# First transfers of a two-layer encoder kernel: order of the first loads, idle products and the list of places

## The chip, the cores and the metric

The kernel runs on one core of a Trainium2 chip. The metric is the device time of one execution in microseconds (us). Before the change the median of three runs is 606.17 us (606.11 to 606.56). The core has five engines with a queue of instructions each: TensorE (PE in the profile, with its weight loads as PEld), VectorE (DVE), ScalarE (ACT), GpSimd (POOL) and SyncE (SP). Each takes its own instructions strictly in the order in which the program was written, and engines wait for each other by semaphores. Transfers between HBM and SBUF are issued by SP and, for the first two of this kernel, by ACT.

## The reference

x is 256 rows of 1024 numbers in fp32. Two layers follow each other, each made of a mixer and a channel sublayer:

```python
def mixer_sublayer(x, n1, w_in_l, ...):
    h = rms_norm(x, n1)
    proj = h @ w_in_l                      # 1024 x 2560
    ...                                    # three attention groups on slices of proj
    return x + mix @ w_out_l
def channel_sublayer(x, n2, w_gu, cw, cb, w_dn):
    h = rms_norm(x, n2)
    g, u = jnp.split(h @ w_gu, 2, axis=-1) # 1024 x 5632
    g = depthwise_conv_centred(g, cw, cb)
    return x + (jax.nn.gelu(g, approximate=False) * u) @ w_dn
```

## The kernel before

Every large product is made from split operands: an fp32 matrix w is held as `hi` (rounded to the PE's fp32r type, by an ACT copy) and `lo` = w - hi (by DVE), and a product is three matmuls, hi by hi, hi by lo and lo by hi (`mm3`). The first products of the program are x (transposed, times the gain of the first norm) by the first slice of `w_in`, called dq: 8 blocks of 128 rows of the weights (k = 0 to 7), for both halves of 128 rows of x (t = 0, 1), three matmuls of 128x384 each: 48 matmuls.

Weights come in units. Unit 0 is blocks k = 0 to 3 of dq, four transfers of one block of 192 KiB each (w0 to w3 below). Unit 1 is blocks k = 4 to 7, in two transfers of 384 KiB (u1a, u1b). Unit 2 (u2) is the first half of the next slice, dk, 768 KiB in one transfer, unit 3 its second half. `load` issues the transfers of a unit, `split` makes its hi and lo. In the order listings below the buffers of the weights are named wp_raw (as loaded), wp_hi and wp_lo; the hi and lo of x transposed are act_hT.

Before the first product x must be turned: `split_T` transposes x on PE (a matmul against the identity `ident`, which is itself loaded), ACT multiplies by the gain and rounds (`hT` hi) and DVE makes the lo. The gain comes from `gl0`, 16x128, which is loaded, transposed on PE against `ident` and copied by DVE (`gains_T`). So the first product needs five things loaded: block 0 of x, `gl0`, `ident` and w0, the last through ACT's copy. x is loaded in blocks of 128 columns of all 256 rows: x0 and x1 alone (by ACT), then in pairs, called here x23, x45 and x67. The table `START` lists these first transfers in the order in which the program records them. While they are under way PE is given products of a constant with itself, whose result nobody reads (`warmed`): `WARM` of them recorded first and `WARM_MORE` wherever PE is free.

The program is not executed as recorded. A class `Plan` records every operation (its number i counts from 0), and `Plan.order` writes the instructions out: again and again it takes, of the operations whose inputs are made by then, the one with the smallest (time it could start, rank, i). The rank is i plus the shifts of the `later` blocks, plus the number that the table `PLACES` gives for i, where it has one. The table's numbers move single operations forward (negative) or back. The times are the planner's own estimates; for the first transfers they are the constants of `LANDS`, taken by the place in `START`.

A transfer gets one of eight semaphores in turn, so that the ninth and each later one is issued only when the transfer eight before it has landed. That wait stands on the issuing engine, and everything behind it in that engine's queue waits too.

Of the kernel before, what the change touches and what calls it, by code (L numbers as in the profile page):

```python
# [11 lines left out]
F32 = mybir.dt.float32  # L12
# [6 lines left out]
P = 128  # L19
# [28 lines left out]


START = [  # L50
    ("act", "x", (0, 1)), ("sync", "g", 0), ("act", "x", (1, 1)), ("sync", "ident", 0), ("sync", "w", 0),
    ("sync", "w", 1), ("sync", "x", (2, 2)), ("sync", "w", 2), ("sync", "w", 3), ("sync", "x", (4, 2)),
    ("sync", "x", (6, 2)), ("sync", "g", 1), ("sync", "g", 2),
]


LANDS = (4100, 3300, 5300, 3450, 5800, 6450, 7250, 8200, 8900, 9800, 10700, 10750, 10800)


WARM, WARM_MORE, WARM_W = 13, 15, 256  # L60

SUM_ACT, SCALE_ACT = ("dq", "dk", "cq"), ("dk",)

# [166 lines left out]
def handover(a, b):  # L230
# [1 line left out]


PLACES = {
# [25 lines left out]
}  # L260


class Plan:
# [83 lines left out]
    def order(self):  # L347
# [7 lines left out]
        free = dict.fromkeys(("ACT", "DVE", "POOL", "SP"), 550.0)  # L355
# [73 lines left out]
        while len(done) < len(ops):  # L429
            best = None  # L430
            for e, r in ready.items():
                for i in r:
                    o = ops[i]
                    if e in opened:
                        if o.burst != opened[e]:
                            continue
                        at = at_of(o)
                    elif o.burst is not None:
                        at = at_of_burst(o.burst) if i == self.bursts[o.burst][0] else None
                    else:  # L440
                        at = at_of(o)
                    if at is not None and (best is None or (at, o.rank, i) < best):
                        best = (at, o.rank, i)
            at, _, i = best
            o = ops[i]
            e = o.engine.name
            ready[e].remove(i)
            done.append(i)
            gone[i] = True
            if o.burst is not None:  # L450
                opened[e] = o.burst
                if i == self.bursts[o.burst][-1]:
                    del opened[e]
            for t in o.tiles:
                if t.slot is None:
                    s = t.pool
                    s.given += 1
                    place = min(s.free)
                    s.free.remove(place)
                    t.since, t.slot = taken_at(place[0], ""), place[1]  # L460
            if e == "PE":
                pe = run_on_pe(o, at)
                end = pe[0] + o.ns + {"turn": 218, "side": 379}.get(o.kind, 163)
            else:
                free[e], end = at + o.ns, at + o.lat
            if o.method == "dma_start":

                ring = e if i < self.first_loads else "SP"
                end = max(at + 1360, wires.get(ring, 0.0))
                shared = 0.0  # L470
                if i < self.first_loads:
                    shared = o.size if ring == "ACT" else min(o.size, 120 * max(0.0, wires.get("ACT", 0.0) - end))
                wires[ring] = end + shared / 120 + (o.size - shared) / (280 if i < self.first_loads else 335)
                end = wires[ring] + 1000
                if i < self.first_loads:
                    end = LANDS[sum(p.method == "dma_start" for p in ops[:i])]
            for t in o.tiles:
                t.left -= 1
                t.until = max(t.until, end)
                t.last[e] = end  # L480
                if not t.left:
                    t.pool.free.append((t.until, t.slot))
            for j in o.after:
                a = ops[j]
                f = a.engine.name
                if e != "PE" or f != "PE":
                    a.at = max(a.at, end + (100 if o.method == "dma_start" else handover(e, f)))
                a.left -= 1
                if not a.left:
                    ready[f].append(j)  # L490
# [55 lines left out]
def encoder_kernel(  # L546
# [27 lines left out]
    act = pool("act", 2)  # L574
    small = pool("small", 4)
    psa = pool("psa", 4, space=bass.MemoryType.PSUM)
    psw = pool("psw", 4, space=bass.MemoryType.PSUM)
# [8 lines left out]
    ident = const.tile([P, P], F32, tag="ident", name="ident")  # L586
# [17 lines left out]

    warm = const.tile([P, P], mybir.dt.bfloat16, tag="warm", name="warm")
    nc.gpsimd.memset(warm, 1.0)
    wps = psw.tile([P, WARM_W], F32, tag="w", name="wps")

    def warmed(n):
        for _ in range(n):  # L610
# [136 lines left out]
    def split_T(srcs, hi, lo, k0, g, name):  # L747


        n = g.shape[1]  # L750
        for b in range(0, n, 2):
            m = min(2, n - b)
            ps = psw.tile([P, 2, S], F32, tag="w", name=f"pt_{name}_{b}")
            for i in range(m):
                k = b + i
                for t in range(NT):
                    nc.tensor.transpose(
                        ps[:, i, t * P : (t + 1) * P], srcs[t][:, k * P : (k + 1) * P], ident
                    )
            for i in range(m):  # L760
                k = b + i
                h, o = hi[:, k0 + k], lo[:, k0 + k]
                nc.scalar.activation(h, ps[:, i], AF.Copy, scale=g[:, k : k + 1])
                nc.vector.scalar_tensor_tensor(
                    o, ps[:, i], g[:, k : k + 1], h.bitcast(F32), ALU.mult, ALU.subtract
                )
# [795 lines left out]
```

## Time and profile before

| | us |
|---|---|
| median of 3 runs | 606.17 |
| the profiled execution | 606.79 |
| its span, first to last instruction | 604.9 |
| PE busy in it | 597.9 |
| first of the 48 dq matmuls starts | 7.50 |
| last matmul of the program ends | 601.41 |

Times in the trace count from the start of the span. A row of the timeline has the start, the duration, the engine, the line (nearly all work has the line of the planner's writer), the operation and its tiles, the number of instructions merged, and in brackets how long the engine had been idle and what it waited for. Of two merged matmuls the second starts before the first one's modelled end, so that the distance of starts says more than the duration.

### The profile page before, as it was taken

What the parts mean: (1) busy time and instruction counts of PE and PEld (TensorE: products, weight loads), DVE (VectorE), ACT (ScalarE), POOL (GpSimd) and SP (SyncE); (2) the same over time, 40 slices, a digit from 0 to 9 for tenths busy, and PEclk for the clock granted to TensorE, in tenths of its full rate; (3) what the DMA queues carried; (4) which work ended last, traced back from release to release, by engine and by line L of the source; (5) the groups of instructions that cost most, each with busy time, mean ns of one, the idle gap of its engine ahead of it and who ended that gap; (6) DMA issues with size and microseconds to landing.
All of it is one profiled execution on the core that took longest, in us unless ns stands there. A gap on an engine that the chain in (4) does not pass through costs nothing.

```text
span 604.9 us, 9691 instructions
## 1 busy us (share of the span) xinstructions
PE 597.9 (99%) x3432; PEld 510.1 (84%) x3432; DVE 462.7 (76%) x951; ACT 426.8 (71%) x1065; POOL 82.5 (14%) x126
## 2 busy tenths in 40 slices
PE   8999999999999999999999999999999999999997
PEld 6998787788888888888899988778888888888886
DVE  4798866889888887878877886557868686777775
ACT  6789999685666676666786998786766556565661
POOL 0733130114300000000023214421000000000000
PEclk9999999999999999999999999999999999999999
DMA  8994123664669899989464817844447374664511
GB/s 269 299 277 168 54 86 109 210 208 141 201 216 306 289 328 319 324 296 310 157 189 137 277 58 256 291 167 138 140 140 254 112 262 139 209 208 161 189 70 70
DMA packets 85218, 121.44 MB, mean 201 GB/s; under 512 B 9881, under 2 KB 69881, under 8 KB 85169
## 3 DMA queue, kind: packets, MB, share of 16 engines
q1 hardware_dynamic: 82896, 112.17, 57.1%
q0 software_dynamic: 1728, 8.39, 4.0%
q8 instruction: 27, 0.44, 0.3%
q10 hardware_dynamic: 544, 0.26, 0.1%
q14 instruction: 23, 0.18, 0.1%
HBM read 110.93 MB, written 9.88 MB: 200 GB/s over the span
## 4 chain that ended last, share of the span: by engine, by line
PE 93%; DMA 2%; issue 1%; DVE 1%; ACT 1%; POOL 1%; SPq 0%; POOLq 0%; DVEq 0%
PE psw_w L498 49%; PE psa_a L498 44%; DMA wp_hi<-dram_khi 1%; DMA wp_raw<-in_w_in_dram 1%; DVE act_z L498 1%; ACT act_hT L498 0%; DVE wp_lo L498 0%; ACT act_s2k L498 0%; ACT wp_hi L498 0%; POOL act_qc L498 0%; POOL act_kc L498 0%; DVE act_sw L498 0%; SPq L498 0%; POOL small_rstd L498 0%; POOL wp_lo L498 0%
## 5 line engine op out<-in xcount | busy, mean ns | idle before, releaser
L498 DVE TENSOR_TENSOR wp_lo<-wp_raw,wp_hi 128x512 fp32r<-128x512 f32 (+2 forms) x332 | 234.9, 736 | 42.3 <-ACT wp_hi L498 21.8
L498 ACT CAST wp_hi<-wp_raw 128x512 fp32r<-128x512 f32 (+2 forms) x332 | 203.0, 666 | 15.7 <-PE psa_a L498 5.6
L498 PE MATMUL psw_w<-act_hT,wp_hi 128*128 128x512 f32 x704 | 181.4, 392 | 0.1
L498 PEld LDWEIGHTS psw_w<-act_hT,wp_hi 128*128 128x128 f32 x704 | 128.6, 188 | 25.1 <-DVE act_hT L498 0.4
L498 PE MATMUL psa_a<-wp_hi,act_hT 128*128 128x384 f32 (+2 forms) x448 | 112.5, 334 | 1.3 <-ACT act_hT L498 1.3
L498 PEld LDWEIGHTS psw_w<-act_hT,wp_lo 128*128 128x128 f32 x704 | 99.0, 190 | 7.7 <-DVE wp_lo L498 0.2
L498 PE MATMUL psw_w<-act_hT,wp_lo 128*128 128x256 f32 x704 | 104.2, 282 | 0.0
L498 PEld LDWEIGHTS psa_a<-wp_hi,act_hT 128*128 128x128 f32 x448 | 77.7, 189 | 4.4 <-ACT act_hT L498 1.6
L498 ACT COPY act_s2k<-psw_w 128x256 f32<-128x256 f32 x88 | 32.5, 373 | 65.6 <-PE psw_w L498 65.5
L498 PE MATMUL psa_a<-wp_lo,act_hT 128*128 128x384 f32 (+2 forms) x224 | 74.6, 336 | 1.1 <-DVE wp_lo L498 1.1
L498 DVE TENSOR_TENSOR act_s2k<-psw_w,act_s2k 128x256 f32<-128x256 f32 x88 | 36.8, 421 | 42.8 <-ACT act_s2k L498 42.1
L498 PE MATMUL psa_a<-wp_lo,act_ch 128*128 128x512 f32 (+1 forms) x176 | 68.7, 393 | 0.0
L498 PE MATMUL psa_a<-wp_hi,act_cl 128*128 128x512 f32 (+1 forms) x176 | 68.3, 392 | 0.0
L498 PE MATMUL psa_a<-wp_hi,act_ch 128*128 128x512 f32 (+1 forms) x176 | 65.7, 393 | 0.0
L498 PEld LDWEIGHTS psa_a<-wp_lo,act_hT 128*128 128x128 f32 x224 | 42.2, 189 | 4.3 <-DVE wp_lo L498 2.3
L498 DVE SCALAR_TENSOR_TENSOR act_s2k<-act_s2k,act_cw,act_s2k 128x255 f32<-128x255 f32 x88 | 38.7, 498 | 0.8 <-ACT act_s2k L498 0.7
L498 PEld LDWEIGHTS psa_a<-wp_lo,act_ch 128*128 128x128 f32 x176 | 33.0, 188 | 7.2 <-DVE wp_lo L498 0.6
L498 PEld LDWEIGHTS psa_a<-wp_hi,act_cl 128*128 128x128 f32 x176 | 33.0, 188 | 7.1
L498 PEld LDWEIGHTS psa_a<-wp_hi,act_ch 128*128 128x128 f32 x176 | 32.7, 188 | 6.4
L498 POOL TENSOR_TENSOR small_rstd<-small_ms,const_mh 128x6 f32<-128x6 f32 (+2 forms) x26 | 33.5, 1287 | 15.9 <-DVE small_ms L498 14.3
L498 ACT ACTIVATE act_s2k<-act_s2k,act_cw 128x256 f32<-128x256 f32 x44 | 24.1, 595 | 15.5 <-DVE act_s2k L498 15.5
L498 ACT ACTIVATE act_s2k<-act_s2k 128x512 f32<-128x512 f32 x22 | 13.9, 632 | 28.6 <-DVE act_s2k L498 28.4
(127 smaller groups left out, 715.6 us busy)
## 6 DMA issues: line engine op xcount, KB each, us to landing
wp_raw<-in_w_gate_up_dram SPq DMA_DIRECT2D x44, 1024.0 KB, 5.2
wp_raw<-in_w_down_dram SPq DMA_DIRECT2D x22, 1024.0 KB, 4.9
wp_raw<-in_w_in_dram SPq DMA_DIRECT2D x14, 768.0 KB, 4.6
wp_raw<-in_w_in_dram SPq DMA_DIRECT2D x8, 1024.0 KB, 6.5
wp_raw<-in_w_out_dram SPq DMA_DIRECT2D x8, 768.0 KB, 6.4
dram_khi<-act_mixT_hi SPq DMA_DIRECT2D x4, 768.0 KB, 6.1
dram_klo<-act_mixT_lo SPq DMA_DIRECT2D x4, 768.0 KB, 9.7
wp_lo<-dram_klo POOLq DMA_DIRECT2D x4, 768.0 KB, 6.0
```

What stands on the lines that cost most here:

```text
L498: getattr(o.engine.real, o.method)(*map(real, o.args), **{k: real(v) for k, v in o.kw.items()})
```

## The change

`START` has the first block of the weights, w0, as SP's first transfer, ahead of `gl0` and `ident`; `LANDS` gives new constants for the planner. `WARM` goes from 13 to 11 and `WARM_MORE` from 15 to 8. The idle products write a PSUM bank of the pool `psa` instead of `psw`. The first four blocks of x are transposed into a PSUM bank each, instead of two blocks to a bank. The planner counts DVE as taken while POOL runs a `tensor_copy`. The list `PLACES` is a new one; only the entries that bear on the opening are shown.

```diff
 START = [
-    ("act", "x", (0, 1)), ("sync", "g", 0), ("act", "x", (1, 1)), ("sync", "ident", 0), ("sync", "w", 0),
+    ("act", "x", (0, 1)), ("sync", "w", 0), ("act", "x", (1, 1)), ("sync", "g", 0), ("sync", "ident", 0),
     ("sync", "w", 1), ("sync", "x", (2, 2)), ("sync", "w", 2), ("sync", "w", 3), ("sync", "x", (4, 2)),
...
-LANDS = (4100, 3300, 5300, 3450, 5800, 6450, 7250, 8200, 8900, 9800, 10700, 10750, 10800)
+LANDS = (3600, 3600, 4500, 3750, 3900, 5200, 5900, 6500, 7000, 7900, 8800, 8850, 8900)
...
-WARM, WARM_MORE, WARM_W = 13, 15, 256
+WARM, WARM_MORE, WARM_W = 11, 8, 256
...
 PLACES = {
-    47: 18, 57: -84, 81: -133, 85: -19, 89: -85, 93: 16, 145: 11, 157: -3, 158: -286, 159: -286, 160: -6, 164: 14,
...
+    76: -251, 77: -166, 78: -166, 80: -153, 82: -153, 120: 6, 137: 110, 159: -236, 160: -236, 161: -236, 189: -272,
...
             else:
                 free[e], end = at + o.ns, at + o.lat
+                if e == "POOL" and o.method == "tensor_copy":
+                    free["DVE"] = max(free["DVE"], at + o.ns)
...
-    wps = psw.tile([P, WARM_W], F32, tag="w", name="wps")
+    wps = psa.tile([P, WARM_W], F32, tag="a", name="wps")
...
         n = g.shape[1]
-        for b in range(0, n, 2):
-            m = min(2, n - b)
+        step = 1 if name == "n100" else 2
+        for b in range(0, n, step):
+            m = min(step, n - b)
```

With nine idle products fewer, operations 76, 77 and 78 of the changed program are the two transfers of unit 1 and the one of unit 2; 80 and 82 are the ACT copies of the first two blocks of unit 1. What the planner makes of it on SP, the first transfers, before (wp_raw_93 is unit 0, wp_raw_130 unit 1, wp_raw_145 unit 2, act_s2k the gains, and a row with x2 stands for two instructions):

```order
L498 DMA act_s2k_81<-in_norm_g_dram 16x128
L498 DMA const_ident_89<-in_c_ident_dram 128x128
L498 DMA wp_raw_93<-in_w_in_dram 128x384 x2
L498 DMA const_x_79<-in_x_dram 128x2x256
L498 DMA wp_raw_93<-in_w_in_dram 128x384 x2
L498 DMA const_x_79<-in_x_dram 128x2x256 x2
L498 DMA act_s2k_122<-in_out_norm_g_dram 16x128
L498 DMA act_s2k_122<-in_norm_g_dram 16x128
L498 DMA wp_raw_130<-in_w_in_dram 128x2x384 x2
L498 DMA wp_raw_145<-in_w_in_dram 128x4x384
```

And on SP in the changed program, from its first transfer (wp_raw_81 is unit 0, wp_raw_88 unit 1, wp_raw_97 unit 2):

```order
L501 DMA wp_raw_81<-in_w_in_dram 128x384
L501 DMA wp_raw_88<-in_w_in_dram 128x2x384 x2
L501 DMA wp_raw_97<-in_w_in_dram 128x4x384
L501 DMA act_s2k_101<-in_norm_g_dram 16x128
L501 DMA const_ident_105<-in_c_ident_dram 128x128
L501 DMA wp_raw_81<-in_w_in_dram 128x384
L501 DMA const_x_79<-in_x_dram 128x2x256
L501 DMA wp_raw_81<-in_w_in_dram 128x384 x2
L501 DMA const_x_79<-in_x_dram 128x2x256 x2
```

Besides w0, all of units 1 and 2 moved ahead of the gains, of `ident`, of w1 to w3 and of x23 to x67.

On ACT, the first work behind its two transfers and the load of its table, before (wp_hi_133 is unit 0, wp_hi_225 unit 1; CAST is the copy to hi, the ACTIVATE on const_x a sum of squares for the norm):

```order
L498 CAST wp_hi_133<-wp_raw_93 128x384
L498 ACTIVATE act_hT_138<-psw_w_116,const_gains_114 128x256 x2
L498 CAST wp_hi_133<-wp_raw_93 128x384
L498 ACTIVATE act_s2k_158,small_ssx_157<-const_x_79 128x512
L498 ACTIVATE act_s2k_169,small_ssx_157<-const_x_79 128x512
L498 CAST wp_hi_133<-wp_raw_93 128x384 x2
L498 ACTIVATE act_hT_138<-psw_w_155,const_gains_114 128x256 x2
L498 ACTIVATE act_hT_138<-psw_w_109,const_gains_114 128x256 x2
L498 ACTIVATE act_s2k_213,small_ssx_157<-const_x_79 128x512
```

And in the changed program at the same place (wp_hi_112 is unit 0, wp_hi_141 unit 1):

```order
L501 CAST wp_hi_112<-wp_raw_81 128x384
L501 ACTIVATE act_hT_131<-psw_w_120,const_gains_127 128x256
L501 ACTIVATE act_hT_131<-psw_w_125,const_gains_127 128x256
L501 CAST wp_hi_141<-wp_raw_88 128x384 x2
L501 CAST wp_hi_112<-wp_raw_81 128x384 x3
L501 ACTIVATE act_hT_131<-psw_w_149,const_gains_127 128x256
L501 ACTIVATE act_hT_131<-psw_w_116,const_gains_127 128x256
L501 ACTIVATE act_s2k_185,small_ssx_184<-const_x_79 128x512
L501 ACTIVATE act_hT_131<-psw_w_120,const_gains_127 128x256 x2
```

Two copies of unit 1 now stand ahead of those of w1 to w3, and the sums of squares behind them.

On PE the changed program has 16 idle products first, then the transposes of the gains, of x0 and, behind one idle product, of x1, two more idle products, and the first four real ones (k = 0, both halves of x); the transposes of x23 follow. Before, 14 idle products stood ahead of the transpose of the gains, 13 more between there and the first real product, and one later.

49 rows, old and new, of the table PLACES are left out of this document.

## The prediction

> **What bounds the kernel.** I read the page's busy times first, then what PE waited for, then the timeline of the opening.
>
> ```profile
> span 604.9 us, 9691 instructions
> PE 597.9 (99%) x3432; PEld 510.1 (84%) x3432; DVE 462.7 (76%) x951; ACT 426.8 (71%) x1065; POOL 82.5 (14%) x126
> PE psa_a L498 <- ACT act_hT L498: 1.3, 1, 1.3
> PE psa_a L498 <- DVE wp_lo L498: 1.1, 2, 0.9
> PE psw_w L498 <- POOL const_mh L498: 1.0, 1, 1.0
> ```
>
> PE is busy 597.9 of 604.9 us, and its waits (total us, times, longest) come to 3.4 us: 1.0 before the first idle product, 1.3 before the first real one, 1.1 in two waits on DVE. What PE does behind its first real product is fixed work, so the end moves with two things: when real products begin and how fast PE then runs. Nothing behind can repay more than 1.1 us and some tenths.
>
> ```profile
> 6.56 0.51 ACT L498 CAST wp_hi<-wp_raw 128x384 fp32r<-128x384 f32 x1 [3.56 <-DMA wp_raw<-in_w_in_dram]
> 6.98 0.84 ACT L498 ACTIVATE act_hT<-psw_w,const_gains 128x256 fp32r<-128x256 f32 x2
> 7.50 0.44 PE L498 MATMUL psa_a<-wp_hi,act_hT 128*128 128x384 f32 x1 [1.29 <-ACT act_hT L498]
> 18.17 0.23 ACT L498 ACTIVATE act_s2k<-psa_a 128x64 f32<-128x64 f32 x1 [0.53 <-PE psa_a L498]
> ```
>
> The first real product starts at 7.50, held by ACT, which was held by w0 until 6.56. ACT waits for the first finished half of dq until 18.17: 10.67 us from the first product to there.
>
> **The order of the transfers** is the term that decides. SP's issues, and for single transfers the time from issue to landing (last number, KB each):
>
> ```profile
> 0.73 0.40 SPq L498 DMA_DIRECT2D act_s2k<-in_norm_g_dram  x1
> 1.18 0.41 SPq L498 DMA_DIRECT2D const_ident<-in_c_ident_dram  x1
> 1.64 0.91 SPq L498 DMA_DIRECT2D wp_raw<-in_w_in_dram  x2
> wp_raw<-in_w_in_dram SPq DMA_DIRECT2D x1, 192.0 KB, 4.9
> 6.56 0.33 SPq L498 DMA_DIRECT2D act_s2k<-in_norm_g_dram  x1
> act_s2k<-in_norm_g_dram SPq DMA_DIRECT2D x1, 8.0 KB, 4.1
> 7.07 2.17 SPq L498 DMA_DIRECT2D wp_raw<-in_w_in_dram  x4
> wp_raw<-in_w_in_dram SPq DMA_DIRECT2D x1, 384.0 KB, 4.3
> ```
>
> So w0 lands at 1.64 + 4.9 = 6.54, the last gains (8 KB, issued 6.56) at 10.66, u1a (issued 7.07) at 11.37. Eight kilobytes need 4.1 us because all that SP issued before goes first. The change puts 192 + 768 + 768 KB (w0, units 1 and 2) ahead of `gl0` and `ident`, so `ident` waits for them. What is moved, in GB/s (the last number, 1000 KB per us):
>
> ```profile
> 1.00:2.00 1.00, 1.00 (x5) 0.70 (x6) 0.00 (x0) 0.28 (x1) 0.00 (x0) 1.00 0.11 32
> 2.00:4.00 2.00, 2.00 (x11) 1.18 (x8) 0.00 (x0) 1.00 (x1) 0.00 (x0) 1.00 0.95 222
> 4.00:6.00 2.00, 2.00 (x19) 1.76 (x18) 0.17 (x1) 0.00 (x0) 0.00 (x0) 1.00 0.83 230
> 6.00:8.00 2.00, 0.71 (x4) 0.46 (x3) 0.71 (x2) 1.44 (x4) 0.00 (x0) 1.00 1.01 340
> 8.00:10.00 2.00, 2.00 (x14) 1.93 (x13) 1.31 (x4) 2.00 (x7) 0.00 (x0) 1.00 0.99 327
> 10.00:12.00 2.00, 2.00 (x17) 1.80 (x16) 1.87 (x5) 1.99 (x6) 0.00 (x0) 1.00 0.96 328
> ```
>
> Up to `ident`, with x0 and x1 (2 x 128 KB on ACT's queue), gains 8 and `ident` 64, that is 2056 KB, or 2105 thousand bytes. By these rows 32 + 444 + 460 + 680 = 1616 are moved by 8.0, and 2105 at 9.5. Landing lags: w0 closes 532 thousand bytes, moved by 4.3 and landed at 6.54 (2.2 later); the last gains close 1925, moved by 8.95, landed 1.7 later; u1a closes 2318, moved by 10.15, landed 1.2 later. So `ident` lands at 9.5 + 1.2 to 1.7, **about 10.8**. From below: if the transfers ran from 2.0 on at the later 330, 2.0 + 2073/330 + 1.2 = 9.5. From above, with w0's lag: 11.7. Before, PE used `ident` at 4.02 (row below).
>
> Behind it come w1 (197 thousand bytes), x23 (262), w2, w3 (197 each), x45 and x67 (262 each): at 330 they land at about 11.4, 12.2, 12.8, 13.4, 14.2 and 15.0. The wait of each for the transfer eight before it (x67 for u2) ends ahead of these times.
>
> **From `ident` to the first product.** PE's clock matters here.
>
> ```profile
> 0.98 3.11 PE L498 MATMUL psw_w<-const_warm 128*128 128x256 bf16 x14 [0.98 <-POOL const_mh L498]
> 4.02 0.23 PE L498 MATMUL psw_w<-const_ident,act_s2k 16*128 16x16 f32 x1
> 4.63 0.71 PE L498 MATMUL psw_w<-const_warm 128*128 128x256 bf16 x5
> 5.18 0.38 PE L498 MATMUL psw_w<-const_ident,const_x 128*128 128x128 f32 x2
> 601.13 0.28 PE L498 MATMUL psw_w<-wp_hi,act_cl 128*128 128x256 f32 x1
> 603.40:604.40 1.00, 0.00 (x0) 0.00 (x0) 0.00 (x0) 0.00 (x0) 0.00 (x0) 1.00 0.00 0
> 604.60:604.90 0.30, 0.00 (x0) 0.00 (x0) 0.00 (x0) 0.00 (x0) 0.00 (x0) 0.58 0.00 0
> ```
>
> The first 14 idle products take (4.02 - 0.98)/14 = 0.217 us each, later ones (5.18 - 4.63)/5 = 0.11: PE runs at half speed for its first 3.1 us. At the end the granted clock (third number from the right) is 1.00 until 604.4 and partly low from 604.6, 3.0 to 3.5 us after the last product's end at 601.41. In the changed kernel the 16 idle products end near 0.98 + 14 x 0.217 + 2 x 0.11 = 4.2, and nothing can follow until 10.8: 6.6 us without work. So PE is slow again. The transpose of the gains (0.23), four of x (two in 0.38 above, which is 0.11 from start to start; 2 x 0.11 each when slow) and three idle products (0.217 each) take 0.23 + 0.88 + 0.65 = 1.8 us, and the first product starts at about **12.6**, 5.1 later. (ACT's hT of x0 is ready before, at 10.8 + 0.7 + 0.45.) From 10.8 another 3.1 us are slow, until 13.9; the 1.3 us of products in it do half their work: **+0.65**.
>
> On what the clock costs there is a page that differs in size. The Trainium skill, TensorE: Matmul & The Clock Gate, Part 1, gives a free-running window of 3.4 us: a whole busy window raises the clock, so the wait for it can be 3.4 to 6.8 us as the phase falls. By it this term would be 0.8 to 2.4 us and the sum 611.2 to 612.8, by the row 611.0; this trace has one such rise, after 3.1 us, and cannot show the spread.
>
> **Is anything later still?** ACT from its first hT on:
>
> ```profile
> L498 ACT CAST wp_hi<-wp_raw 128x384 fp32r<-128x384 f32 x12 | 5.6, 514 | 4.0 <-DMA wp_raw<-in_w_in_dram 4.0
> L498 ACT ACTIVATE act_hT<-psw_w,const_gains 128x256 fp32r<-128x256 f32 x8 | 3.5, 473 | 0.0
> L498 ACT ACTIVATE act_s2k<-const_x 128x512 f32<-128x512 f32 x4 | 2.5, 635 | 0.0
> 15.88 1.76 ACT L498 CAST wp_hi<-wp_raw 128x384 fp32r<-128x384 f32 x4 [0.44 <-DMA wp_raw<-in_w_in_dram]
> 16.06 0.51 PE L498 MATMUL psa_a<-wp_hi,act_hT 128*128 128x384 f32 x2
> 16.41 0.33 PE L498 MATMUL psa_a<-wp_lo,act_hT 128*128 128x384 f32 x1
> ```
>
> The same 24 instructions stand there, one CAST of them ahead (w0's, early now): 5.6 x 11/12 + 3.5 + 2.5 = 11.1 us, from 11.5 to 22.6, where before the last CAST of unit 2 ended at 17.64: 5.0 later. In ACT's queue the CASTs of w1 to w3 hold the hT of x23 until about 14.5, w3 having landed at 13.4. PE, from 12.6, needs 0.65 + 10.67 us to the end of the first half of dq: 23.9, so PE's sum and ACT's agree to within a microsecond, and PE's is the later. The early landing of units 1 and 2 gains nothing: they were not waited for long (0.44 above).
>
> **Other parts.** Nine idle products fewer cost nothing: all but one stood in a wait, and the wait is longer now. Separate banks for x0 to x3 and `psa` for the idle products cost nothing on PE: no instruction is added, and the banks are free until the first product. The new list moves work all along. What it can gain is the wait behind POOL's copy:
>
> ```profile
> 21.38 1.84 POOL L498 COPY act_nab<-act_few 28x1984 f32<-28x1984 f32 x1
> 21.93 3.38 DVE L498 TENSOR_TENSOR wp_lo<-wp_raw,wp_hi 128x384 fp32r<-128x384 f32 x4
> 23.69 0.45 PE L498 MATMUL psa_a<-wp_lo,act_hT 128*128 128x384 f32 x1 [0.88 <-DVE wp_lo L498]
> ```
>
> Four of DVE's lo take 3.38 us beside the copy, and PE waits 0.88. In the changed program the copy stands seven POOL instructions later, and the planner keeps DVE's work off it. Bounds: 0.9 gained (the wait is gone), 0.9 lost (a second such wait, as the opening's real times aren't those planned for). I take **-0.9**, as the list was made with that rule.
>
> **Sum.** Against the profiled execution's 606.79 (span 604.9 and 1.9 around it): 5.1 + 0.65 - 0.9 = +4.85, 611.6. The median of the runs is 0.6 below the profiled one, so the forecast is 606.17 + 4.85 = **611.0**.
>
> **Rivals.** (1) *Transfers under way share the engines*, so a small one overtakes. `ident`, SP's sixth issue at 0.73 + 5 x 0.45 = 3.0, would land as x0 did, 2.5 us after its issue:
>
> ```profile
> const_x<-in_x_dram ACTq DMA_DIRECT2D x2, 128.0 KB, 2.5
> ```
>
> That is 5.5; the first product would start near 6.6, 0.9 earlier, PE's clock would hold, and with -0.9 the time is 604.4. It decides below about 7.5 for the first product. Against it: the 8 KB that took 4.1. The Trainium skill, DMA: Bandwidth & Descriptors, Queues, rings and completion order, has each engine take descriptors in ring order, though a later one may finish its write first. 7%. (2) *The delay is repaid* to within 0.2%: `ident` would have to land by about 7.3, between the two cases, or PE save 3.6 us more where it waits 1.1. 3%, 606.5. (3) *The clock stays low* in the opening, because PE now waits between products for ACT: some 20 more of the 48 products at twice their 0.175 us ((16.41 - 16.06)/2, above) add 3.5, giving 614.5. 8%. (4) *The clock holds* through the gap: the first product at 11.9 (ACT's hT), no slow products: 4.4 - 0.9, 609.7. 12%. The forecast has 70%.
>
> **Range and chances.** Lower end: `ident` at 9.5 instead of 10.8 and the clock partly kept: 611.0 - 1.3 - 1.3 = 608.4. Upper: `ident` at 11.7 and no gain at POOL's copy, 611.0 + 0.9 + 0.9 = 612.8, and part of rival 3, 613.4. Outside are rivals 1 and 2 and most of 3, some 18%. A measurement can tell 0.2%, 1.2 us, from no change; faster 0.07, same 0.03, slower 0.90.
>
> **What would show it.** The gains and `ident` landing near 10.8 and the transpose of the gains right behind; an idle stretch of PE of over 6 us from about 4.2; a granted clock below 1.00 in 8 to 13; the first real product near 12.6; ACT's first sums of dq near 23.5; no PE wait of 0.9 on DVE beside POOL's copy. A first product before 7.5 would make the prediction wrong from its root.

## The result and the profile after

Timed side by side on one chip, the changed kernel takes 611.21 us (median of four, 611.08 to 611.87) and the one before 606.14 (605.53 to 606.56): a ratio of 1.0087, 95% interval 1.0069 to 1.0104, that is 4.2 to 6.3 us slower. The forecast was 611.0.

The page of the changed kernel, its span and the busy times:

```profile
span 609.3 us, 9680 instructions
PE 598.8 (98%) x3423; PEld 512.1 (84%) x3423; DVE 461.3 (76%) x951; ACT 424.4 (70%) x1065; POOL 80.4 (13%) x126
```

The span is 4.4 us longer, and PE is busy only 0.9 us longer although it has nine matmuls fewer. So PE waits more. All its waits (total us, times, longest):

```profile
PE psw_w L501 <- DMA const_ident<-in_c_ident_dram: 4.8, 1, 4.8
PE psa_a L501 <- POOL const_mh L501: 1.0, 1, 1.0
PE psa_a L501 <- DVE wp_lo L501: 0.7, 1, 0.7
PE psw_w L501 <- DVE act_z L501: 0.2, 1, 0.2
```

The 1.3 us for ACT's hT are gone, and 4.8 for `ident` stand in their place. The opening in the timeline (start, duration, engine, line, operation, tiles, count, idle time before):

```profile
0.73 1.89 SPq L501 DMA_DIRECT2D wp_raw<-in_w_in_dram  x4
2.66 0.50 SPq L501 DMA_DIRECT2D act_s2k<-in_norm_g_dram  x1
3.20 0.42 SPq L501 DMA_DIRECT2D const_ident<-in_c_ident_dram  x1
...
0.98 3.60 PE L501 MATMUL psa_a<-const_warm 128*128 128x256 bf16 x16 [0.98 <-POOL const_mh L501]
9.39 0.26 PE L501 MATMUL psw_w<-const_ident,act_s2k 16*128 16x16 f32 x1 [4.81 <-DMA const_ident<-in_c_ident_dram]
...
10.98 0.67 PE L501 MATMUL psa_a<-wp_hi,act_hT 128*128 128x384 f32 x1
11.45 0.52 PE L501 MATMUL psa_a<-wp_lo,act_hT 128*128 128x384 f32 x1
11.77 0.52 PE L501 MATMUL psa_a<-wp_hi,act_hT 128*128 128x384 f32 x1
...
13.03 0.95 PE L501 MATMUL psa_a<-wp_hi,act_hT 128*128 128x384 f32 x4
13.82 0.34 PE L501 MATMUL psa_a<-wp_lo,act_hT 128*128 128x384 f32 x1
...
22.47 0.22 ACT L501 ACTIVATE act_s2k<-psa_a 128x64 f32<-128x64 f32 x1 [1.80 <-PE psa_a L501]
...
605.48 0.28 PE L501 MATMUL psw_w<-wp_hi,act_cl 128*128 128x256 f32 x1
```

Against the rows of before: the first real product starts at 10.98 instead of 7.50 (+3.48), the first half of dq ends at 22.47 instead of 18.17 (+4.30), and the last matmul starts at 605.48 instead of 601.13 (+4.35). The whole loss is there after 22 us; behind, next to nothing is lost or repaid on balance. (The end of the first half of dq is read from ACT's first sum over it, `act_s2k<-psa_a`, as in the prediction.) The products from 11.45 on start 0.32 us apart, those from 13.03 on (13.82 - 13.03)/4 = 0.20: PE's clock was low until about 12.9. `ident` in the chain that ended last (start, duration):

```profile
3.20 6.05 DMA const_ident<-in_c_ident_dram
```

64 KB, issued at 3.20, landed at 9.25.

### The profile page after: what moved, and what is told of

It reads as the page before. It is cut to its first block, busy times and chain, and to the rows that moved or that the text cites. A ratio compares the mean times of both kernels' runs of the same rounds, so it can differ in the third digit from the quotient of the medians.

```text
span 609.3 us, 9680 instructions
## 1 busy us (share of the span) xinstructions
PE 598.8 (98%) x3423; PEld 512.1 (84%) x3423; DVE 461.3 (76%) x951; ACT 424.4 (70%) x1065; POOL 80.4 (13%) x126
## 4 chain that ended last, share of the span: by engine, by line
PE 92%; DMA 2%; DVE 2%; POOL 1%; issue 1%; ACT 1%; SPq 0%; POOLq 0%; ACTq 0%
PE psw_w L501 50%; PE psa_a L501 42%; DMA wp_lo<-dram_klo 1%; DMA const_ident<-in_c_ident_dram 1%; POOL small_rstd L501 1%; DVE wp_lo L501 1%; SPq L501 0%; DVE act_z L501 0%; DVE const_x L501 0%; ACT act_s2k L501 0%; ACT act_z L501 0%; POOL small_ms L501 0%; ACT wp_hi L501 0%; DVE act_sw L501 0%; POOL act_cdq L501 0%
## 5 line engine op out<-in xcount | busy, mean ns | idle before, releaser
L501 PE MATMUL psa_a<-wp_hi,act_ch 128*128 128x512 f32 (+1 forms) x176 | 68.3, 392 | 0.0
L501 DVE SCALAR_TENSOR_TENSOR act_s2k<-act_s2k,act_cw,act_s2k 128x255 f32<-128x255 f32 x88 | 37.2, 479 | 2.1 <-ACT act_s2k L501 2.0
L501 POOL TENSOR_TENSOR small_rstd<-small_ms,const_mh 128x6 f32<-128x6 f32 (+2 forms) x26 | 32.2, 1238 | 15.6 <-DVE small_ms L501 14.0
```

What stands on the lines that cost most here:

```text
L501: getattr(o.engine.real, o.method)(*map(real, o.args), **{k: real(v) for k, v in o.kw.items()})
```

## The experiments

Those that move transfers without a new plan do it where the instructions are written out; `made` is that order, and the operations named by number are moved ahead of another. For each the ratio to the kernel before is given; the kernel before had a median of 607.03 beside the first four, 606.33 beside the two with the undone opening's hole filled and with nine idle products fewer, and 606.2 beside the others.

**The kernel before, with only units 1 and 2 (and w0) ahead of the gains and `ident` on SP** (34 is w0, 85 to 87 the transfers of units 1 and 2):

```diff
-            for i in self.order():
+            made = [i for i in self.order() if i not in [34, 85, 86, 87]]
+            at = made.index(31)
+            made[at:at] = [34, 85, 86, 87]
+            for i in made:
```

> The kernel before with one thing moved: on SP w0 and units 1 and 2 are issued first, everything else in its old order, with its old list and 28 idle products. Theory A: ident lands near 9.3, the first real product starts near 11, the clock is low at first, and the time is 610.2 us (609.3 to 611.3), most of the change's loss. Rivals B and C: without fewer idle products and without the new list no loss, 606.1 (605.5 to 606.8).

1.0102 [1.0086, 1.0118]. From its timeline and its windows (window, its length, busy time of the engines, granted clock third from the right, DMA share, GB/s):

```profile
9.90 0.26 PE L501 MATMUL psw_w<-const_ident,act_s2k 16*128 16x16 f32 x1 [5.75 <-DMA const_ident<-in_c_ident_dram]
13.55 0.67 PE L501 MATMUL psa_a<-wp_hi,act_hT 128*128 128x384 f32 x1
```

```profile
7.50:10.80 3.30, 0.90 (x5) 0.83 (x6) 0.61 (x2) 0.00 (x0) 0.00 (x0) 0.50 1.08 379
10.90:14.20 3.30, 3.30 (x17) 2.66 (x15) 0.67 (x2) 1.55 (x4) 0.00 (x0) 0.50 0.89 285
```

The order of the transfers alone makes the whole loss and more (1.0102 where 610.2 us, some 1.007, were expected): the same wait for `ident`, and behind it the 13 idle products of before, now at half speed (clock 0.50), hold the first product until 13.55. From the use of `ident` to the first product it takes 3.65 us here and 1.59 in the changed kernel, which has three idle products there; ten idle products more at about 0.21 us account for the difference. By this estimate the fewer idle products spare the changed kernel some 2 us.

**The changed kernel without the three entries that move units 1 and 2 forward**, planned again:

```diff
-    76: -251, 77: -166, 78: -166, 80: -153, 82: -153, 120: 6, ...
+    80: -153, 82: -153, 120: 6, ...
```

> The changed kernel without the three entries of the list that move units 1 and 2 ahead. Theory A (the place of units 1 and 2 ahead of ident is the whole cost): ident lands near 3.9 instead of 9.25, the first real product starts at 5.0 to 5.6 (before 7.50, changed 10.98), PE's clock is full there, and the time is about 603.9 us (602.8 to 605.2), faster than both. Rival B (nine idle products fewer, so a cold PE, is the cost): the clock comes late here too and the time stays above 608. Rival C (the rest of the new list costs): 606.5 to 609.

1.0010 [0.9997, 1.0023]. The loss is gone. The gain that was expected is not there, though the opening is early. Its timeline:

```profile
6.36 0.44 PE L501 MATMUL psa_a<-wp_hi,act_hT 128*128 128x384 f32 x1
18.70 0.23 ACT L501 ACTIVATE act_s2k<-psa_a 128x64 f32<-128x64 f32 x1 [2.08 <-PE psa_a L501]
```

The first product is 1.14 us earlier than in the kernel before, the end of the first half 0.53 later: PE has waits in between (0.7 for ACT's hi, 0.4 for x) and work that the list places ahead.

**The changed kernel with the gains and `ident` right behind w0, units 1 and 2 behind these**, but still ahead of w1 to w3 and x23 to x67:

```diff
+            made = [i for i in self.order() if i not in [24, 25]]
+            at = made.index(76)
+            made[at:at] = [24, 25]
```

> The changed kernel with only the gains and ident (72 KB) issued right behind w0, units 1 and 2 still ahead of w1 to w3 and the rest of x. Theory A with the whole order as cause: the first real product starts near 5.3, but after four of them PE waits for x23, which lands at about 10.3 as in the changed kernel, so that only 1.2 to 2.2 us come back: 609.5 us (608.8 to 610.2). If ident alone is the cost, nearly all comes back: 606.5 to 607.3.

1.0083 [1.0065, 1.0102]: nothing gained, where 1.2 to 2.2 us were expected. In its timeline the wait has moved:

```profile
6.11 0.44 PE L504 MATMUL psa_a<-wp_hi,act_hT 128*128 128x384 f32 x1
...
11.51 1.12 PE L504 MATMUL psw_w<-const_ident,const_x 128*128 128x128 f32 x4 [4.43 <-DMA const_x<-in_x_dram]
```

Four products at 6.11, then 4.43 us for x23, which stands behind the same 1536 KB. In that wait the clock fell (0.50 from 10.8 to 14.2), so that the products behind it are slow as well, and the first half of dq ends at 22.58. So `ident` is only the first of the things that are late; what costs is that the two units go ahead of *anything* the first products need.

**The kernel before with the new `START` and `LANDS` only**, its old list kept and planned with them:

```diff
-    ("act", "x", (0, 1)), ("sync", "g", 0), ("act", "x", (1, 1)), ("sync", "ident", 0), ("sync", "w", 0),
+    ("act", "x", (0, 1)), ("sync", "w", 0), ("act", "x", (1, 1)), ("sync", "g", 0), ("sync", "ident", 0),
```

> The kernel before with the new START and LANDS alone, its own list, 28 idle products, old banks. Theory A: w0 as SP's first transfer is good in itself; first real product at 5.2 to 6.0, time 604.3 us (603.4 to 605.3). If w0 ahead of ident is itself what hurts, ident lands over a microsecond later and the time is 606 or more.

1.0052 [1.0035, 1.0069], expected faster: missed. The opening is early (first half of dq at 17.32, 0.85 before the old one), the last matmul at 604.70, 3.57 later. Of PE's waits that are new against the kernel before these are the longest:

```profile
PE psw_w L498 <- ACT act_s2k L498: 0.9, 2, 0.5
PE psa_a L498 <- DMA wp_hi<-dram_khi: 0.6, 1, 0.6
PE psa_a L498 <- ACT wp_hi L498: 0.6, 1, 0.6
PE psw_w L498 <- DMA const_x<-in_x_dram: 0.5, 1, 0.5
```

They are spread over the first 400 us. The list of numbers was made for the old times of the planner; with others it puts work in other places all along. The next run, which leaves the order as planned before, bears out that this costs more here than w0 first does. So a new plan can't tell what a new opening is worth.

**The kernel before with only w0 at the head of SP's queue**, written out otherwise as it was:

```diff
+            made = self.order()
+            for what, ahead_of in [([34], 31)]:
+                made = [i for i in made if i not in what]
+                at = made.index(ahead_of)
+                made[at:at] = what
...
```

> The kernel before as written out, with only w0 moved to the head of SP's transfers; nothing is planned anew. If the opening's gain is real and the loss of the replanned run (START alone) came from its list no longer fitting: first real product near 6.4, first half of dq done at 17.0 to 17.5 (before 18.17), ratio 0.998 to 0.999. If w0 first is no gain: first half of dq at 18.2 and ratio 1.000; if it hurts by itself, ratio over 1.002 and 610 us as in the replanned run.

1.0015 [1.0003, 1.0028]. In the profiled execution PE is early for a long time (first product at 6.71, first half of dq at 17.48, 0.69 early), and then:

```profile
395.39 0.30 PEld L506 LDWEIGHTS psa_a<-wp_hi,act_mixT_hi 128*128 128x128 f32 x2 [1.34 <-DMA wp_hi<-dram_khi]
```

The weight load waits 1.34 for a block of weights that POOL reloads. In the kernel before it stood at the same place, at nearly the same time, with a shorter wait:

```profile
395.45 0.30 PEld L498 LDWEIGHTS psa_a<-wp_hi,act_mixT_hi 128*128 128x128 f32 x2 [0.58 <-DMA wp_hi<-dram_khi]
```

The reload in the chain that ended last (start, duration), before, in this run, and in the run with nine idle products fewer (below):

```profile
389.10 6.30 DMA wp_hi<-dram_khi
388.28 7.07 DMA wp_hi<-dram_khi
390.22 7.07 DMA wp_hi<-dram_khi
```

POOL issued it 0.82 earlier, and it took 0.77 longer, so that it landed no sooner; the last matmul starts at 601.00, 0.13 early. In that profile the early start is used up there. The longer transfer is no consequence of being early: it takes 7.07 us also where PE comes late. Why is open. By the ratio the kernel is 0.9 us slower than the one before (medians 607.69 and 606.20), which the trace doesn't explain: its eleven executions fall into two groups, five from 606.05 to 606.57, the profiled one among them, and six from 607.69 to 608.72, and no trace was taken of the second. It stays open.

**The changed kernel with the opening undone in the written order**: units 1 and 2 behind the first loads again, ACT's and DVE's work on u1a behind that on w1 to w3, nothing planned anew.

```diff
+            made = self.order()
+            for what, ahead_of in [([80, 81, 82, 83], 129), ([76, 77, 78], 79)]:
+                made = [i for i in made if i not in what]
+                at = made.index(ahead_of)
+                made[at:at] = what
...
```

> The changed kernel as written out, with only this moved: on SP units 1 and 2 stand behind the other first transfers again (the order of START), and ACT's and DVE's first two pieces of unit 1 behind w1 to w3 and x23 to x67. All other instructions keep the changed kernel's order, so that the list's effect on the rest stays. Theory A (the whole loss is the place of units 1 and 2): first real product at 5.8 to 6.5, first half of dq done near 17 instead of 22.5, ratio to before 0.997 to 0.999. Rival C (the new list loses elsewhere, as the replanned run of the changed list might say): ratio 1.000 to 1.004 with the opening as early.

1.0028 [1.0017, 1.0039]; last matmul at 602.79, 2.69 earlier than in the changed kernel. Some 3 us (2.7 by the profile, 0.0059 or 3.6 us by the ratios) come back with nothing but these seven operations moved. More was expected by theory A: the first product comes at 7.27 and the first half of dq ends at 20.15, not near 17. What remains shows in its timeline:

```profile
0.99 3.60 PE L509 MATMUL psa_a<-const_warm 128*128 128x256 bf16 x16 [0.99 <-POOL const_mh L509]
5.68 0.25 PE L509 MATMUL psw_w<-const_ident,act_s2k 16*128 16x16 f32 x1 [1.10 <-DMA const_ident<-in_c_ident_dram]
...
7.74 0.52 PE L509 MATMUL psa_a<-wp_lo,act_hT 128*128 128x384 f32 x1
8.06 0.52 PE L509 MATMUL psa_a<-wp_hi,act_hT 128*128 128x384 f32 x1
```

PE has a hole of 1.10 us, and its products are 0.32 apart behind it.

**The same with that hole filled**: the sixteenth idle product six times.

```diff
-                getattr(o.engine.real, o.method)(...)
+                idle += o.method == "matmul" and o.args[1].dtype == mybir.dt.bfloat16
+                for _ in range(6 if idle == 16 and o.method == "matmul" and ... else 1):
+                    getattr(o.engine.real, o.method)(...)
```

> The opening of the change undone as in the run that undid it (units 1 and 2 and ACT's two pieces behind again; that left 1.0028 [1.0017, 1.0039]), and now the sixteenth idle product of the list 6 times, 5 more of about 0.22 us, so that PE bridges the 1.1 us for which it waited for ident there. Theory (what was left of the loss is the clock, which came full only at 9.83): full clock by 4 to 5 us, first product of weights at 7.0 to 7.5, end of the first half of dq 18.9 to 19.4 where it was 20.15, last matmul 601.5 to 602.1 where it was 602.79; ratio 1.0005 to 1.0020. Rival (the rest of the loss is the new list, made for other starts): clock early too, but the last matmul within 0.3 of 602.79 and ratio 1.0025 to 1.0035.

1.0016 [1.0007, 1.0025]. Its timeline:

```profile
0.98 3.83 PE L512 MATMUL psa_a<-const_warm 128*128 128x256 bf16 x21 [0.98 <-POOL const_mh L512]
...
6.21 0.44 PE L512 MATMUL psa_a<-wp_hi,act_hT 128*128 128x384 f32 x1
6.49 0.34 PE L512 MATMUL psa_a<-wp_lo,act_hT 128*128 128x384 f32 x1
6.67 0.35 PE L512 MATMUL psa_a<-wp_hi,act_hT 128*128 128x384 f32 x1
...
19.59 0.23 ACT L512 ACTIVATE act_s2k<-psa_a 128x64 f32<-128x64 f32 x1 [2.09 <-PE psa_a L512]
```

The clock is high for the first products (0.18 apart), and the first one comes 1.06 us earlier than without the filling; of that only 0.56 arrive at 19.59 and 0.58 at the last matmul (602.21). But this pair doesn't show that the filling did it. PE uses `ident` at 5.08 here and at 5.68 there, though SP issues it at 1.63 in both; that is 0.60 of the 1.06. And the clock rose here before the two programs differ: the starts of the idle products are 0.21 apart up to 3.73 and 0.11 from 3.89 on, while the added ones begin behind 4.0; without the filling all sixteen were slow (3.60/16 = 0.225), and the rise came at 9.83. The intervals of the two ratios overlap. PE, early now, waits for x:

```profile
PE psw_w L512 <- DMA const_x<-in_x_dram: 1.2, 1, 1.2
```

The ratio is the theory's, the last matmul lies between theory and rival, and neither is shown. About 1.1 us against the kernel before stay, and all of it is lost by 19.59 (18.17 before): the new order asks for x sooner than it lands and waits 0.4 for ACT's hi. How much of it is the list's and how much the other parts of the change (the order of `START`, the banks), no run separates.

**The changed kernel with its own hole filled**: the sixteenth idle product 49 times, so that PE works up to `ident`.

```diff
+                for _ in range(49 if idle == 16 and o.method == "matmul" and ... else 1):
```

> The changed kernel with the 16th idle product of PE issued 49 times instead of once, so that PE stays busy until ident is there (48 more at 0.11 to 0.21 us, to 9.4 to 11). Theory: about 1 us of the loss is PE's low clock behind the gap; with it full from ident on, the first half of dq is done 0.5 to 1.5 us earlier than 22.47 and the ratio to before falls from 1.0087 to 1.006 to 1.008. If the clock costs nothing there, because ACT's 10 us of work set the pace, the ratio stays at 1.0087 and dq at 22.3 to 22.5.

1.0066 [1.0052, 1.0079]; first product at 10.60, those behind it 0.17 apart, and:

```profile
21.68 0.23 ACT L504 ACTIVATE act_s2k<-psa_a 128x64 f32<-128x64 f32 x1 [1.61 <-PE psa_a L504]
```

That is 0.79 us earlier than in the changed kernel, 0.62 at the last matmul (604.86). So the low clock is 0.6 to 0.8 us of the 4.35 in the profiles; the intervals of the two ratios overlap. Here too the clock rose before the programs differ (at 3.8), but that alone would not have kept it: with units 1 and 2 first in the kernel before it rose at 4.0 and fell again in the wait for `ident`.

**The kernel before with nine idle products fewer** (one of those ahead of `ident`, eight of those behind):

```diff
+            idle = [i for i in made if self.ops[i].method == "matmul" and ...]
+            gone = set(idle[13:14] + idle[18:26])
+            for i in [i for i in made if i not in gone]:
...
```

> The kernel before with nothing changed but nine idle products fewer: one of the fourteen ahead of ident and eight of those between x's transposes and the first products. Theory (the shorter run of idle products is no part of the 5 us so long as the clock still comes full before the first products, and the first product waits for hT and w0's parts and not for PE): first product 7.2 to 7.5 where it was 7.50, full clock by 3.9 to 7.3, last matmul within 0.5 of 601.13; ratio 0.999 to 1.001. Rival (the clock goes down in the gap that they leave, or comes up a period of 3.4 us later): products 0.32 apart until 7.3 or longer, last matmul 0.5 to 1.3 later, ratio 1.001 to 1.002.

1.0004 [0.9995, 1.0013]: no difference in the medians. But the profiled execution is the slowest of its eleven (608.50, the others 605.46 to 607.39), and its windows say why in part:

```profile
3.80:7.20 3.40, 1.50 (x12) 1.00 (x11) 0.64 (x2) 1.01 (x3) 0.00 (x0) 1.00 0.88 277
...
7.30:10.60 3.30, 3.30 (x12) 3.19 (x13) 2.37 (x5) 3.30 (x10) 0.00 (x0) 0.50 1.05 363
...
10.70:14.00 3.30, 3.30 (x24) 3.10 (x23) 1.75 (x5) 1.88 (x6) 0.00 (x0) 1.00 1.04 378
```

PE worked 1.50 of the 3.4 us from 3.8 on (a wait of 1.9 for ACT's hT is among them), the clock went to 0.50 (narrower windows put the fall at 7.28 and the rise at 10.69, 3.41 us), and the first half of dq ended 1.10 later (19.27), the last matmul 1.80 (602.93). The other 0.70 come from the reload, which took 7.07 us instead of 6.30. In the kernel before the same wait is 1.29 and the clock held. So the idle products do work: they cost nothing and keep a dip of about one us from happening in some executions. The mean granted clock, which is on record for every execution, shows in which ones: 3.41 us at half speed take 0.003 off it. It is 0.996 or 0.997 in three of the eleven, the longest ones (607.02, 607.39 and 608.50), and 0.999 or 1.000 in the eight others (605.46 to 606.80), as it is in all 55 executions of the kernel before that stood beside the experiments.

**The changed kernel with POOL's copy in eight pieces** of 28x248, so that DVE can get in between:

```diff
...
+                if o.engine.name == "POOL" and o.method == "tensor_copy":
+                    for c in range(0, GRID_W, 8):
+                        o.engine.real.tensor_copy(args[0][:, c : c + 8], args[1][:, c : c + 8])
+                    continue
...
```

> The changed kernel with POOL's copy of 28x1984 in eight pieces of 28x248. In the changed kernel one lo of DVE takes 1.89 us beside the copy instead of 0.55, and PE waits 0.72 for it. If DVE is kept out for the length of one POOL instruction, the pieces let it in between: that lo takes under 1.0 us, PE's wait is under 0.2, and the ratio falls by about 0.001. If DVE is merely slowed by POOL's reading, the lo still takes 1.5 us or more.

1.0119 [1.0099, 1.0138], slower. First the changed kernel's own rows around the copy, then those of this one:

```profile
30.17 1.83 POOL L501 COPY act_nab<-act_few 28x1984 f32<-28x1984 f32 x1
30.53 1.89 DVE L501 TENSOR_TENSOR wp_lo<-wp_raw,wp_hi 128x384 fp32r<-128x384 f32 x1
32.47 0.44 PE L501 MATMUL psa_a<-wp_lo,act_hT 128*128 128x384 f32 x1 [0.72 <-DVE wp_lo L501]
```

```profile
30.54 4.05 POOL L504 COPY act_nab<-act_few 28x248 f32<-28x248 f32 x8
...
30.90 0.78 DVE L506 TENSOR_TENSOR wp_lo<-wp_raw,wp_hi 128x384 fp32r<-128x384 f32 x1
```

The lo that took 1.89 beside the whole copy takes 0.78 beside the pieces, and PE's longest wait for a lo goes from 0.7 to 0.3. So it is the one long POOL instruction that holds DVE. But the eight pieces take 4.05 us instead of 1.83, and PE now waits 1.4 on DVE's act_z in three waits; the last matmul is 1.67 later, 0.38 of which were there ahead of the copy, as `ident` came later (9.78 instead of 9.39).

## Why the prediction was right, point by point

- **`ident` at 10.8, because units 1 and 2 go first: the mechanism right, the size 1.55 too large.** The two runs that move these transfers in the written order, in either direction (with w0 1.0102 from the kernel before; with ACT's and DVE's first work on unit 1 from 1.0087 back to 1.0028), show the mechanism. It landed at 9.25. The step that was mis-sized is the rate: I used the rows of before, 230 GB/s from 4 to 6 us. The changed kernel's windows:

```profile
2.00:4.00 2.00, 2.00 (x12) 1.42 (x10) 0.00 (x0) 1.39 (x2) 0.00 (x0) 1.00 0.82 248
4.00:6.00 2.00, 0.58 (x3) 0.10 (x1) 0.56 (x1) 0.15 (x1) 0.00 (x0) 1.00 1.09 378
6.00:8.00 2.00, 0.00 (x0) 0.00 (x0) 0.00 (x0) 0.00 (x0) 0.00 (x0) 1.00 1.04 366
```

  With 30 thousand bytes moved by 2.0, these rows reach the 2105 thousand that `ident` closes at about 8.2 instead of 9.5, and it landed 1.0 later, where I took 1.2 to 1.7. Even the lower bound of 9.5 was too late.
- **From `ident` to the first product 1.8 us**: 1.73 measured. So the first product came +3.48 late, predicted +5.1.
- **Low clock, +0.65**: it was low until about 12.9, 3.5 us behind the first transpose (predicted 3.1). From the first product to the end of the first half of dq PE took 22.47 - 10.98 = 11.49 us instead of 10.67, +0.82. In the new order 51 products stand in this stretch and in the old 49 and an idle one, so that some 0.2 are not the clock's; about 0.6 are, and with the hole filled the end comes 0.62 to 0.79 earlier. Here the Trainium skill, TensorE: Matmul & The Clock Gate, Part 1, gave an estimate of 0.8 to 2.4 us by its free-running window of 3.4 us (2.5 by the prediction's own figures, (6.8 - 1.8)/2); the trace lies at or below the lower end of that. The length of its window agrees: the low stretch in the kernel with fewer idle products is 3.41 us. The same section of the Trainium skill lets the clock fall after an idle window; there it fell after one in which PE was busy 1.50 of 3.4 us, and the measurement decides.
- **ACT's work agrees with PE's sum, PE's is later**: so it was; ACT stood 1.80 us idle for PE ahead of 22.47. PE's sum was 1.4 too late (23.9) and ACT's 1.9 (22.6; ACT was done at 20.67), by `ident` above all.
- **The wait beside POOL's copy gone, -0.9**: wrong. In the new order one lo beside the copy remained instead of four, it took 1.89, and PE waits 0.72 for it instead of 0.88: a gain of 0.16. I had taken the upper of the two ends that I gave; the value lies between them, near nothing.
- **The rest of the list nothing**: from 22.47 to the end the difference goes from 4.30 to 4.35. With the 0.16 gained and the two products more ahead of 22.47, some 0.4 are lost elsewhere in it. This holds for the late opening only: with the opening undone and the hole filled about 1.1 us are lost, in the first 20 us.
- **The sum**: +4.85 forecast; 3.48 + 0.82 + 0.05 = +4.35 by the profiles. That the time itself came out within 0.3 us is luck, for errors cancel: `ident` was overrated by 1.6, the gain at POOL's copy by 0.74, and some 0.4 lost elsewhere were not foreseen; and the medians stand 5.07 apart where the profiled executions stand 4.29 apart, as that of before (606.79) lies above its other runs and that of the changed kernel (611.08) is the lowest of its four.
- **The rivals**: that transfers share the engines so that `ident` overtakes is refuted (it needed 6.05 us, not 2.5). That the clock holds is refuted (0.32 apart). That it stays low through the opening is refuted (13.03). Nothing was repaid.
- Of the signs, the idle stretch of PE was to be over 6 us from about 4.2 and was 4.8 from 4.58, since `ident` came sooner and all sixteen idle products ran slow. One sign was useless: "a granted clock below 1.00 in 8 to 13". The windows of the changed kernel say 1.00 there and PE ran at half speed, and so do those of the kernel before for its first idle products. The column showed low values only behind an earlier rise; at a program's start the distance between starts of matmuls of one width shows the clock.

No version tried was faster than the kernel before.

## What to carry to other kernels

In this kernel a transfer's place in the queue was its time. Count the bytes ahead of the *last* small thing that the first product needs, and do it for each of these things, since moving one of them up only hands the wait to the next. Weights that are needed only later may stand early in a plan and still cost their whole transfer time. A list of places made for one set of planned times is not to be judged, nor used, with another: w0 first gave 1.0052 with a new plan and 1.0015 with the old order kept. And an opening that was 0.7 us early in the trace didn't reach the end: a single transfer that took 0.77 us longer, 390 us later, was as large. One profile before and one after can't tell differences of this size apart; `ident`, issued at 1.63 in six of these kernels, was used between 4.63 and 5.68.

## What was not expected of the hardware

- The transfers ran at 366 to 378 GB/s from 4 to 8 us in the changed kernel, while the kernel with units 1 and 2 behind (1.0010) moved much less from 4 to 6:

```profile
4.00:6.00 2.00, 1.64 (x10) 1.09 (x9) 0.73 (x2) 0.23 (x2) 0.00 (x0) 1.00 0.95 181
```

  The kernel before has 230 there. In the four kernels with the 1536 KB ahead of the gains and `ident` the rate is 356 to 378, in the eight others 179 to 241; in the one of these with the two small transfers right ahead of the 1536 KB it is 181. Why is open; an estimate of a landing must not take its rate from another order of transfers.
- PE's clock changed in steps of 3.41 us whose phase differs from one execution to another, by the traces' record of it. In the three traces with several changes these stand at 3.87, 7.28 and 10.69 (nine idle products fewer), 4.04, 7.45 and 14.28 (the kernel before with units 1 and 2 first) and 3.98, 10.81 and 14.22 (`ident` right behind w0): 3.41 or twice that apart. In all twelve traces PE's work begins at 0.98 or 0.99; the first rise came between 3.8 and 4.1 in six of them, between 4.6 and 5.7 in three and between 9.8 and 13.4 in the three others, among them the changed kernel. Reckoned in such steps back and forth from these changes, the clock rose behind steps in which PE was busy 2.7 us or more and not behind those with 2.31 or less; once up, it fell behind those with 1.51 (the wait of 1.9 us) or less and held with 2.20 or more (in the kernel before 2.32, with the wait of 1.29).
- A POOL copy in eight pieces costs 4.05 / 8 = 0.51 us each, 2.2 us more in all than the whole.
